# A two-layer hybrid encoder: both layers' Hyena filter networks on two halves of the partitions, and layer 1's decay table made at the end of layer 0

## The chip, the core and the metric

One NeuronCore of one Trainium2 chip runs the whole program. Its engines are TensorE (PE, the matrix products; PEld is its weight load), VectorE (DVE), ScalarE (ACT), GpSimd (POOL) and SyncE (SP, which here only issues DMAs). Each of them works through its own queue in order: an instruction that waits holds up all that stand behind it on the same engine. The metric is device time in microseconds (us) of one execution, lower is better.

## What is computed

The reference runs two layers over two independent requests (s = 0 and 1, 512 tokens of 1024 features each) that share all weights. Cut to what matters here:

```python
def _layer(x, p, ...):
    h = _rmsnorm(x, norm_mix)
    q, k, v, g, hy_in, pool_in = jnp.split(h @ w_in, ...)
    ret = _retention(_rope(q), _rope(k), v, ret_decay_fwd, ret_decay_bwd)   # 4 heads
    ret = _head_layernorm(ret, ret_gn) * jax.nn.silu(g)
    hy_out = _hyena(hy_in, ..., hy_w1, hy_b1, hy_freq, hy_w2, hy_b2, hy_w3, hy_bias)
    pool_out = _pool_mixer(pool_in, pool_w, pool_scale)
    x = x + jnp.concatenate([ret, hy_out, pool_out], axis=-1) @ w_out
    gate, up = jnp.split(_rmsnorm(x, norm_ffn) @ ffn_w_up, 2, axis=-1)
    x = x + (jax.nn.gelu(_dwconv3(gate, ffn_conv)) * up) @ ffn_w_down
    return x + jax.nn.sigmoid(x @ ple_gate_w) * _rmsnorm(p @ ple_w, ple_norm)

def _hyena_filters(L, w1, b1, freq, w2, b2, w3):      # depends on the weights of the layer alone
    h = jnp.sin(fr * (feats @ w1 + b1))               # 512 x 33 @ 33 x 64
    h = jnp.sin(fr * (h @ w2 + b2))                   # 512 x 64 @ 64 x 64
    h = (h @ w3).reshape(L, HY_ORDER, 2, HY_WIDTH) * jnp.exp(-t * deltas)
    k_full = ...; k_full = k_full / jnp.sum(jnp.abs(k_full), axis=0)
    return jnp.fft.rfft(k_full, axis=0)

def _retention(q, k, v, logit_f, logit_b):
    lgf, lgb = log_sigmoid(logit_f), log_sigmoid(logit_b)
    dmask = exp(dist * lgf) below the diagonal, exp(dist * lgb) above     # the decay table
    ...
```

The filters and the decay table of a layer hang on weights alone, so they can be made at any time before the layer uses them.

## The kernel before

Activations lie feature-major, in tiles of 128 features by 512 tokens. A large product splits weights and activations into a high and a low fp16 part and makes three matmuls per 128x128 block (`mm3`, L322 to L324; `pass3`, L327 to L329, for products of activations). Weights come by DMA as `wraw`, and ACT and DVE split them into `wspl` (one instruction on each).

The program is recorded from generators ("threads"): one main thread per request (projections named `q0`..`q3`, `k`, `g`, `hy0`..`hy5`, `pl0`, `pl1`, the output projections `o0`..`o7`, the gated FFN `fg`, `fu`, then a joint FFN `fx`, `fy`, `fz` of both requests, and the per-layer embedding with `pe` and the gate products `s0`..`s7`), one thread per retention head (`sc` scores, `st`/`pt` decayed scores, `ov`, then a head norm with `cs` column sums and `rb` their broadcast), per pooling block (`pu`, `pw`, `pm`, `pq`), per Hyena request, and for each layer one filter thread and one decay thread. `schedule()` steps the thread whose planned time is due; a thread's `ready` is such a planned time, in planned microseconds. What comes out sets the order on PE and on SP. The order on DVE, ACT and POOL is chosen by a list scheduler when the program is built. On the chip all of them are fixed queues.

The two side threads that the change touches:

- `filter_thread(l)`: loads `feats`, the small weights `fw` and `w3`; two products (`fp<-feats,fw` L468 and `fp<-fa,fw` L474, each in 32 bits), each followed by five to seven DVE instructions and a Sin on ACT (`sine`, names `fa`, `sk`); the split `h2`; eight products `fp<-w3s,h` that make `hfb`, `fabs`, `fs`, `fd`, `ftot`; then the sum `fp<-ftot,ones` (L510), its reciprocal `frec` (L512), a block of folds (`fold`, `fold1`, `folds`) and the spectrum products `khat`. Layer 0's thread runs at the start of the program. Layer 1's is spawned when request 0 reaches `pl1` (`EARLY`) in layer 0, and so runs beside the second half of layer 0's mixer.
- `decay_thread(l)`: loads four tables `dpm`, takes `log_sigmoid` of eight numbers (24 DVE instructions on 128x8 and an Exp `yy`), and for eight half tables makes `dect` (two DVE instructions, an Exp on ACT, a store `ddec`). Heads load it back as `dec`.

Sigmoid, Exp, Sin and Gelu need different tables in ACT: a change of function shows as an ACT_TABLE_LOAD.

Of the kernel before, what the change touches and what calls it, by code (L numbers as in the profile page):

```python
# [31 lines left out]
JOINT = 3  # L32
HYW = 256
# [15 lines left out]
EARLY = "pl1"  # L49

# [46 lines left out]
def tile_order():  # L97

    names = ["v00", "v01", "v10", "v11"]
    for h, more in enumerate((["hy0", "hy1", "hy2", "hy3"], ["hy4", "hy5", "pl0"], ["pl1"], [])):  # L100
        names += [f"q{h}", f"k{h}", f"g{h}"] + more
    names += [f"o{m}" for m in range(NB)]
    for j in range(PLAIN):
        names += [f"fg{j}", f"fu{j}"]
    tiles, steps = list(names), list(names)
    pairs = []
# [15 lines left out]
    return tiles + more, steps + more  # L122
# [13 lines left out]


TILES, STEPS = tile_order()
TILE_AT = {n: i for i, n in enumerate(TILES)}
STEP_AT = {n: i for i, n in enumerate(STEPS)}  # L140
NT, NS = len(TILES), len(STEPS)


class Trunk:
# [54 lines left out]
    def plan_weights(self):  # L199
# [3 lines left out]
        for i in range(self.depth * NS):  # L203
            l, name = divmod(i, NS)
            name = STEPS[name]
# [24 lines left out]
    def prep(self, i):  # L230

        while self.wnext < self.need[i]:
            assert self.room()
            self.piece()
        k = i
        while k + 1 < len(self.at):

            frm = min(self.pos) if "." in STEPS[(k + 1) % NS] else i
# [16 lines left out]
    def wtile(self, l, last):  # L255
        self.live.append(l * NS + STEP_AT[last])
        return self.wp.tile([128, 2, 1024], F16, tag="wspl", name="wspl")
# [7 lines left out]
    def raw_names(self, j):  # L265

        return ("fg" + j[1:], "fu" + j[1:]) if j[0] == "f" else ("ea" + j[1:], "eb" + j[1:])
# [40 lines left out]
    def weight(self, l, name, *ss):  # L308
        i = l * NS + STEP_AT[name]
# [122 lines left out]
    def sine(self, a):  # L432

        k = self.g(name="sk")[0:64, :]
# [13 lines left out]
    def filter_thread(self, l, ev):  # L448
        nc, io = self.nc, self.io
        ft = self.g(name="feats")  # L450
        self.load(ft[0:33, :], io["feats"])
        fw = self.g(name="fw")
        self.load(fw[0:64, 0:132], io["fw"][l])
        w3 = []
        for o in range(2):
            w = self.g(name="w3")
            self.load(w[0:64, :], io["w3"][l][:, o * T:(o + 1) * T])
            q = self.g([128, 2, T], F16, name="w3s")
            self.split(q[0:64, 0], q[0:64, 1], w[0:64, :], WS)
# [4 lines left out]
        w1, w2, b1, fr, b2 = fw[0:33, 0:64], fw[0:64, 64:128], fw[0:64, 128:129], fw[0:64, 129:130], fw[0:64, 130:131]  # L464
# [7 lines left out]
        a2 = self.g(name="fa2")  # L472
        p = self.bank(name="fp")
        nc.tensor.matmul(p[0:64, :], w2, a[0:64, :], start=True, stop=True)  # L474
        self.ts(a2[0:64, :], p[0:64, :], b2, fr, ALU.add, ALU.mult)
        self.sine(a2[0:64, :])
        a = None
        h2 = self.g([128, 2, T], F16, name="h2")
        self.split(h2[0:64, 0], h2[0:64, 1], a2[0:64, :])
        yield 0.9, LAT["sin"][l > 0]  # L480
# [380 lines left out]
    def main_thread(self, s):  # L861
# [12 lines left out]
        for l in range(self.depth):  # L874
            vec = self.vec[l]
            h = []
            yield from self.h_steps(s, x, acc, vec[:, V_NMIX:V_NMIX + NB], h)
            x = None
            if s == 0 and l > 0:
                yield [self.ffn[l - 1].over]  # L880
            hw = self.hcw[l]
            mix = [None] * NB
            done = []
            hy, hev = [], [Event() for _ in range(6)]
            v = []
            for name in TILES[:TILE_AT["o0"]]:
                if name[0] == "v":
                    if name[2] == "0":
                        v.append([])
                        ps = self.values_early(l, h, s) if name == "v00" else [None, None]  # L890
                        for tp in range(2):
                            self.values(l, int(name[1]), h, s, tp, v[-1], ps.pop(0))
                            if ps or name != "v00":
                                yield (10.4 if name == "v00" else 5.2), 0.0
                    continue
                if name == "q0" and s == 0 and l > 0:
                    self.load_rope()
                if name == EARLY and s == 0 and l + 1 < self.depth:
                    self.spawn(self.filter_thread(l + 1, self.khat_ev[l + 1]))
                p = self._proj(l, name, h, s)  # L900
                if name[:2] == "hy":
                    if name == "hy0" and s == 0:
                        self.load_dft(l)
                    j = int(name[2])
                    hy.append(self.conv3(p, hw, j, 6))
                    yield 5.15, 0.0
                    hev[j].set(self.clock + 3.0)
                    if j == 0:
                        done.append(Event())
                        self.spawn(self.hyena_thread(l, hy, hev, mix, done[-1]))  # L910
                elif name[:2] == "pl":
                    b = int(name[2])
                    if b == 0:
                        pw = self.g(name="poolw")
                        self.load(pw[:, 0:256], io["poolw"][l])
                    rc = self.g(name="rc")
                    self.load(rc, io["rcnt"][b])
                    m = self.pooling(p, b, rc)
                    yield 5.15, 0.0
                    done.append(Event())  # L920
                    self.spawn(self.pool_thread(l, b, m, None, pw[:, b * 128:(b + 1) * 128], mix, done[-1]))
                elif name[0] == "q":
                    qk = {"q": self.rotate(p)}
                    yield 5.15, 0.0
                elif name[0] == "k":
                    qk["k"] = self.rotate(p)
                    yield 5.15, 0.0
                else:
                    hd = int(name[1])
                    sg = self.g(name="sg")  # L930
                    self.act(sg, p, ACTF.Sigmoid, scale=1.0 / WS)
                    self.stt(sg, p, 1.0 / WS, sg, ALU.mult, ALU.mult)
                    if hd == 0:
                        yield [self.decay_ev[l]]
                    dec = self.dp.tile([128, 896], F32, tag="dec", name="dec")
                    nc.sync.dma_start(out=dec, in_=self.ddec[l, hd])
                    yield 5.15, 0.0
                    done.append(Event())
                    self.spawn(self.head_thread(l, hd, qk, v, sg, dec, mix, done[-1]))
            h = None  # L940
            if s == 1:
                self.rope = None
            yield done
# [96 lines left out]


# [64 lines left out]
    def ffn_joint(self, l, f):  # L1106

        nc, fcw = self.nc, self.fcw[l]
        b11, b21, b22 = f.h[0][0:4], f.h[0][4:8], f.h[1][4:8]
        t1, t2, t3, t4 = f.sums  # L1110
        f.h = f.sums = None
        right = (b11, t1, b21, t2, b22, t3, t4)
        state = {}
        first = STEP_AT[f"f{PLAIN}.0"]
        end = STEP_AT[f"d{len(PARTS) - 1}_0"]
# [362 lines left out]
```

## Time and profile before

| | |
|---|---|
| time, median of 3 runs | 2456.72 us (2451.26 to 2456.94) |
| the profiled execution's own time | 2451.95 us |
| its span, first to last instruction | 2450.2 us |
| mean granted TensorE clock | 0.990 |
| busy PE / DVE / ACT / POOL | 2379.1 / 1779.5 / 1032.3 / 700.8 us |

PE is busy for 97% of the span, so the time is PE's work plus the few places where PE waits. A wait in a row of the timeline stands in brackets behind the instruction that waited: the idle time before it, and what ended it. PEclk in the table of windows is the granted clock as a share of 2.4 GHz: 0.50 is 1.2 GHz.

### The profile page before, as it was taken

The page shows a single profiled execution, that of the slowest core. Times are in us where ns is not written, and L with a number is a line of the kernel's source. Part 1 is how long each engine was busy: PE and PEld are TensorE (multiplying, and loading weights), DVE is VectorE, ACT ScalarE, POOL GpSimd, SP SyncE. Part 2 cuts the span into 40 slices and gives each one's busy share as a digit, 9 for nine tenths or more (in the row PEclk, how much of TensorE's full clock was granted, in tenths as well). Part 3 has the DMA queues.
Part 4 walks back from the last instruction along what each step waited for, and adds up shares of the span by engine and source line. Part 5 has one row for each costly group of instructions (what it writes and reads, how often), then busy time and mean ns, then how long its engine had stood idle before and what let it go on. Part 6 is the DMA issues. An engine that isn't in the chain of part 4 may idle for free.

```text
span 2450.2 us, 30877 instructions
## 1 busy us (share of the span) xinstructions
PE 2379.1 (97%) x12024; PEld 1169.9 (48%) x12024; DVE 1779.5 (73%) x2526; ACT 1032.3 (42%) x1551; POOL 700.8 (29%) x528
## 2 busy tenths in 40 slices
PE   5999989999999999999999999999999999999997
PEld 4544654444444444444456555544444444444443
DVE  7994886968877868866575686554987786886655
ACT  4543334445534435444433343333553543544441
POOL 1213244124233333320121222510423334332011
PEclk8999999999999999999999999999999999999998
DMA  6122020341121121113232111032012112121301
GB/s 226 65 98 63 24 75 21 115 139 38 45 65 59 46 71 53 62 48 112 78 120 108 50 49 53 28 115 65 27 48 65 58 46 69 54 63 48 112 1 69
DMA packets 64363, 168.60 MB, mean 69 GB/s; under 512 B 7574, under 2 KB 13718, under 8 KB 64216
## 3 DMA queue, kind: packets, MB, share of 16 engines
q1 hardware_dynamic: 58312, 156.40, 19.3%
q10 hardware_dynamic: 5904, 10.23, 1.1%
q8 instruction: 94, 1.54, 0.3%
q14 instruction: 53, 0.43, 0.1%
HBM read 152.18 MB, written 14.42 MB: 68 GB/s over the span
## 4 chain that ended last, share of the span: by engine, by line
PE 74%; DVE 13%; issue 3%; ACT 2%; POOL 2%; DMA 0%; POOLq 0%; DVEq 0%; SPq 0%; ACTq 0%
PE fx L1183 13%; PE ex L1183 7%; PE fy L1183 7%; PE ey L1183 4%; PE fz L1183 3%; PE s L322 2%; PE o L323 2%; PE o L324 2%; PE o L322 2%; PE s L323 2%; PE s L324 2%; PE ez L1183 2%; DVE t L174 2%; DVE wspl L171 2%; DVE conv L171 2%
## 5 line engine op out<-in xcount | busy, mean ns | idle before, releaser
L1183 PEld LDWEIGHTS <-wspl 128*128 128x128 f16 x4704 | 461.1, 98 | 566.2 <-issue 13.7
L174 POOL TENSOR_TENSOR wraw<-wraw 128x512 f32<-128x512 f32 (+1 forms) x240 | 344.4, 1435 | 654.8 <-DVE wspl L171 640.7
L168 ACT ACTIVATE wspl<-wraw 128x1024 f16<-128x1024 f32 (+2 forms) x360 | 327.1, 910 | 370.8 <-POOL wraw L174 71.1
L171 DVE SCALAR_TENSOR_TENSOR wspl<-wraw,wspl 128x1024 f16<-128x1024 f32 (+2 forms) x360 | 395.5, 1100 | 82.6 <-ACT wspl L168 81.3
L1183 PE MATMUL fx<-hs,wspl 128*128 128x512 f16 x1368 | 312.3, 382 | 7.7 <-ACT r L168 7.7
L322 PEld LDWEIGHTS <-wspl 128*128 128x128 f16 x1536 | 152.1, 99 | 181.2 <-issue 6.9
L324 PEld LDWEIGHTS <-wspl 128*128 128x128 f16 x1536 | 150.6, 98 | 183.3 <-issue 3.3
L323 PEld LDWEIGHTS <-wspl 128*128 128x128 f16 x1536 | 150.7, 98 | 177.3 <-issue 3.6
L1183 PE MATMUL ex<-at,wspl 128*128 128x512 f16 x846 | 192.7, 379 | 0.0
L174 POOL TENSOR_TENSOR y<-t,mhalf 128x4 f32<-128x4 f32 x30 | 36.3, 1210 | 402.6 <-DVE t L178 402.5
L168 ACT ACTIVATE at<-conv 128x512 f16<-128x512 f32 x142 | 89.4, 629 | 143.7 <-DVE conv L174 111.8
L174 DVE TENSOR_TENSOR at<-conv,at 128x512 f16<-128x512 f32 x142 | 127.1, 896 | 26.2 <-ACT at L168 24.8
L171 DVE SCALAR_TENSOR_TENSOR conv<-r,scaled,conv 128x511 f32<-128x511 f32 x152 | 129.5, 852 | 2.1 <-ACT conv L168 0.4
L1183 PE MATMUL fx<-h,wspl 128*128 128x512 f16 x456 | 104.6, 379 | 0.0
L1183 PE MATMUL fy<-hs,wspl 128*128 128x512 f16 x456 | 104.6, 379 | 0.0
L1183 PE MATMUL fz<-h,wspl 128*128 128x512 f16 x456 | 104.6, 379 | 0.0
L1183 PE MATMUL fy<-h,wspl 128*128 128x512 f16 x456 | 104.6, 379 | 0.0
L168 ACT ACTIVATE sq<-x 128x512 f32<-128x512 f32 x80 | 49.2, 625 | 123.4 <-DVE x L171 66.3
L1183 PE MATMUL ey<-at,wspl 128*128 128x512 f16 x432 | 101.1, 379 | 0.0
L168 ACT ACTIVATE conv<-conv 128x512 f32<-128x512 f32 x88 | 55.3, 629 | 108.2 <-DVE conv L171 107.1
L174 DVE TENSOR_TENSOR acc<-acc,sq 128x512 f32<-128x512 f32 x84 | 62.6, 747 | 48.5 <-ACT sq L168 47.3
L324 PE MATMUL s<-xs,wspl 128*128 128x512 f16 x256 | 97.0, 379 | 0.0
(246 smaller groups left out, 4662.8 us busy)
## 6 DMA issues: line engine op xcount, KB each, us to landing
wraw<-in_w SPq DMA_DIRECT2D x172, 512.0 KB, 3.8
wraw<-in_w SPq DMA_DIRECT2D x48, 384.0 KB, 3.0
x<-in_x SPq DMA_DIRECT2D x32, 256.0 KB, 4.3
dec<-ddec SPq DMA_DIRECT2D x16, 448.0 KB, 4.6
wraw<-in_w SPq DMA_DIRECT2D x16, 256.0 KB, 2.6
xsp<-x ACTq DMA_DIRECT2D x16, 256.0 KB, 2.0
x<-xsp SPq DMA_DIRECT2D x16, 256.0 KB, 5.0
out_y<-out SPq DMA_DIRECT2D x16, 256.0 KB, 2.8
```

Source lines behind the costliest of these rows:

```text
L168: return self.nc.scalar.activation(out=out, in_=in_, func=func, **k)
L171: return self.nc.vector.scalar_tensor_tensor(out=out, in0=in0, scalar=scalar, in1=in1, op0=op0, op1=op1)
L174: return (eng or self.nc.vector).tensor_tensor(out=out, in0=in0, in1=in1, op=op)
L322: self.nc.tensor.matmul(out, wv[:, 0, kb, :], x[:, 0], start=first, stop=False)
L323: self.nc.tensor.matmul(out, wv[:, 0, kb, :], x[:, 1], start=False, stop=False)
L324: self.nc.tensor.matmul(out, wv[:, 1, kb, :], x[:, 0], start=False, stop=last)
L1183: mm = lambda a, b, start=False, stop=False: self.nc.tensor.matmul(out, a, b, start=start, stop=stop, skip_group_check=not first)
```

## The change

Layer 0's filter thread now makes the inner layers of both layers: layer 0 stands on partitions 0 to 63 and layer 1 on 64 to 127 (`fw` holds the two `w1` side by side and the two `w2` as a block diagonal), so the two products and the sines have 128 rows and as many columns as before, and `h2` stays in SBUF until layer 1's thread uses its lower half. Layer 1's filter thread is still spawned at `EARLY`, but begins with the `w3` products. Layer 1's decay thread gets the planned time 25 + 1125 in place of 25 + 400. A main thread that reaches its first head gate no longer gives way to others when the decay table is already there. The bodies of the projections' steps move into a function `take`. The diff also adds a way of running pairs of projections jointly (`TWINS`, `mix_joint`, `rights`); `TWINNED` is empty, so that code is never entered.

```diff
+TWINNED = ()
 EARLY = "pl1"
+LATER = 1125.0
...
     def sine(self, a):
-        k = self.g(name="sk")[0:64, :]
+        k = self.g(name="sk")
...
     def filter_thread(self, l, ev):
         nc, io = self.nc, self.io
-        ft = self.g(name="feats")
-        self.load(ft[0:33, :], io["feats"])
-        fw = self.g(name="fw")
-        self.load(fw[0:64, 0:132], io["fw"][l])
+        rows = slice(l * 64, (l + 1) * 64)
+        if l == 0:
+            ft = self.g(name="feats")
+            self.load(ft[0:33, :], io["feats"])
+            fw = self.g(name="fw")
+            self.load(fw[:, 0:259], io["fw"])
...
-            self.split(q[0:64, 0], q[0:64, 1], w[0:64, :], WS)
+            self.split(q[rows, 0], q[rows, 1], w[rows, :], WS)
...
-        a = self.g(name="fa")
-        p = self.bank(name="fp")
-        nc.tensor.matmul(p[0:64, :], w1, ft[0:33, :], start=True, stop=True)
-        self.ts(a[0:64, :], p[0:64, :], b1, fr, ALU.add, ALU.mult)
-        self.sine(a[0:64, :])
-        yield 0.9, LAT["sin"][l > 0]
...
+        if l == 0:
+            w1, w2, b1, fr, b2 = fw[0:33, 0:128], fw[:, 128:256], fw[:, 256:257], fw[:, 257:258], fw[:, 258:259]
+            a = self.g(name="fa")
+            p = self.bank(name="fp")
+            nc.tensor.matmul(p, w1, ft[0:33, :], start=True, stop=True)
+            self.ts(a, p, b1, fr, ALU.add, ALU.mult)
+            self.sine(a)
+            yield 0.9, LAT["sin"][0]
...
+            self.h2 = self.g([128, 2, T], F16, name="h2")
+            self.split(self.h2[:, 0], self.h2[:, 1], a2)
+            yield 0.9, LAT["sin"][0]
+        h2 = self.h2
...
-                self.pass3(p, h2[0:64, 0, jj], h2[0:64, 1, jj], w3[o][0:64, 0], w3[o][0:64, 1], True, True)
+                self.pass3(p, h2[rows, 0, jj], h2[rows, 1, jj], w3[o][rows, 0], w3[o][rows, 1], True, True)
...
-                    if hd == 0:
-                        yield [self.decay_ev[l]]
...
+            if hd == 0 and self.decay_ev[l].time is None:
+                yield [self.decay_ev[l]]
...
-            self.spawn(self.decay_thread(l, self.decay_ev[l])).ready = 25.0 + 400.0 * l
+            self.spawn(self.decay_thread(l, self.decay_ev[l])).ready = 25.0 + LATER * l
...
-    fw = np.zeros((depth, 64, 132), f4)
+    fw = np.zeros((128, 259), f4)
```

Three places show how the queues move. The first is PE, layer 0, where `pl1` of request 0 ends; before, what stands behind its last matmul is the first of the two small filter products, and then the scores of the next head:

```order
L324 MATMUL pl_3193<-h,wspl 128x512
L468 MATMUL fp<-feats,fw 64x512
L327 LDWEIGHTS qk
L327 MATMUL sc<-qk 128x512
L328 LDWEIGHTS qk
```

And now (L339 to L341 are the three passes of `pass3`):

```order
L336 MATMUL pl_3193<-h,wspl 128x512
L339 LDWEIGHTS h_530
L339 MATMUL fp<-w3s,h_530 128x512
L340 LDWEIGHTS h_530
L340 MATMUL fp<-w3s,h_530 128x512
L341 LDWEIGHTS h_530
L341 MATMUL fp<-w3s,h_530 128x512
L339 LDWEIGHTS qk
L339 MATMUL sc<-qk 128x512
```

The first `w3` product stands where the feature product stood, and it reads `w3s`, which ACT and DVE make. The second place is DVE in layer 0 right after `pl1` of request 1. Before, two heads' decayed scores stand there between the last filter products' sums:

```order
L174 TENSOR_TENSOR qk<-rt,qk 128x512
L174 TENSOR_TENSOR fs_3674<-hfb 128x256
L174 TENSOR_TENSOR fd_3678<-hfb 128x256
L171 SCALAR_TENSOR_TENSOR st<-sc,dec 128x512
L174 TENSOR_TENSOR ftot<-ftot,fabs 128x256
L171 SCALAR_TENSOR_TENSOR st<-sc,dec 128x512
```

Now the reciprocal (L529, directly behind the two `wspl` that stand there), the first head's four `st` and four `pt`, and these rows stand there, ahead of the second head's `st` and `pt`:

```order
L186 TENSOR_TENSOR qk<-rt,qk 128x512
L540 COPY fold_3919<-fold 128x512
L186 TENSOR_TENSOR fold<-fold,frec 128x512
L543 COPY fold<-fd_3258 1x512
L186 TENSOR_TENSOR fold<-fold,frec 128x512 x2
L541 COPY fold_3919<-fold 1x512
L186 TENSOR_TENSOR fold<-fold,frec 128x512 x4
L542 COPY fold<-fs_3252 1x512
L186 TENSOR_TENSOR fold_3919<-fold_3919,frec 128x512
L183 SCALAR_TENSOR_TENSOR st<-sc,dec 128x512
L183 SCALAR_TENSOR_TENSOR folds<-fold,folds 128x512
L186 TENSOR_TENSOR fold<-fold,frec 128x512
```

Before, the reciprocal and this block stood behind the last heads' scores, beside `o0` to `o2`. The third place is ACT at the end of layer 0, from the gate of product `s6` of request 0 to that of `s2` of request 1. Before:

```order
L168 ACTIVATE sg<-s_10223 128x512
L168 ACTIVATE wspl<-wraw 128x1024
L168 ACTIVATE sq<-x 128x512
L184 DMA xsp<-x 128x512 x2
L168 ACTIVATE sq<-x 128x512
L184 DMA xsp<-x 128x512
L168 ACTIVATE sg<-s_10284 128x512
```

And now, behind the gate of `s6`:

```order
L180 ACT_TABLE_LOAD
L180 ACTIVATE dect<-dect 128x448
L196 DMA ddec<-dect 128x448
L180 ACTIVATE wspl<-wraw 128x1024
L180 ACTIVATE dect<-dect 128x448
L196 DMA ddec<-dect 128x448
L180 ACTIVATE sq<-x 128x512
L196 DMA xsp<-x 128x512 x2
L180 ACTIVATE sq<-x 128x512
L196 DMA xsp<-x 128x512
L180 ACT_TABLE_LOAD
L180 ACTIVATE sg<-s_10233 128x512
```

Exp and Sigmoid now alternate there: the program has 22 ACT_TABLE_LOADs in place of 15, three fewer in the mixer of layer 0 and ten more in this stage.

## Rows read from the trace of the kernel before

**Rows 1.** The page, part 1: busy time, share of the span, instructions.
```profile
PE 2379.1 (97%) x12024; PEld 1169.9 (48%) x12024; DVE 1779.5 (73%) x2526; ACT 1032.3 (42%) x1551; POOL 700.8 (29%) x528
```

**Rows 2.** Timeline of PE, its waits: start us, us, instruction, [idle before, releaser].
```profile
44.87 1.87 PE L753 MATMUL cs<-ones,acc 128*128 128x1 f32 x8 [6.57 <-DVE acc L174]
...
333.42 0.38 PE L324 MATMUL pl<-h,wspl 128*128 128x512 f16 x1
333.63 0.38 PE L322 MATMUL pl<-h,wspl 128*128 128x512 f16 x1
...
334.37 1.07 PE L468 MATMUL fp<-feats,fw 33*64 33x512 f32 x2
...
359.26 1.05 PE L753 MATMUL cs<-ones,sq 128*128 128x1 f32 x8 [2.48 <-ACT sq L168]
...
398.08 0.39 PE L327 MATMUL fp<-w3s,h 64*128 64x512 f16 x1
...
422.36 1.05 PE L753 MATMUL cs<-ones,sq 128*128 128x1 f32 x8 [2.75 <-ACT sq L168]
...
466.25 0.56 PE L763 MATMUL rb<-identr,rr 128*128 128x128 f16 x7 [1.33 <-DVE rr L171]
...
1246.30 0.95 PE L753 MATMUL cs<-ones,acc 128*128 128x1 f32 x8
...
1279.41 1.02 PE L753 MATMUL cs<-ones,acc 128*128 128x1 f32 x8 [0.50 <-DVE acc L174]
```

**Rows 3.** Windows: us, then busy time of each engine, PEclk, DMA share, GB/s.
```profile
37.60:51.30 13.70, 7.13 (x35) 5.23 (x34) 12.95 (x25) 4.07 (x7) 2.04 (x1) 0.50 0.55 200
...
423.30:426.70 3.40, 3.40 (x10) 1.17 (x11) 3.16 (x10) 1.81 (x3) 2.13 (x2) 0.50 0.66 217
...
500.00:600.00 100.00, 100.00 (x485) 46.87 (x484) 75.86 (x102) 43.80 (x72) 35.84 (x26) 1.00 0.26 86
```

**Rows 4.** Timeline, behind `pl1` of request 0: the split of `w3`.
```profile
334.97 1.14 ACT L168 ACTIVATE w3s<-w 64x512 f16<-64x512 f32 x2
...
335.62 1.14 DVE L171 SCALAR_TENSOR_TENSOR w3s<-w,w3s 64x512 f16<-64x512 f32 x1 [2.23 <-ACT w3s L168]
```

**Rows 5.** Timeline of DVE, from `pl1` of request 1 to the folds.
```profile
399.76 1.25 DVE L171 SCALAR_TENSOR_TENSOR wspl<-wraw,wspl 128x1024 f16<-128x1024 f32 x1 [1.28 <-ACT wspl L168]
...
406.15 1.77 DVE L174 TENSOR_TENSOR pt<-st,pt 128x512 f16<-128x512 f32 x1
...
415.46 0.69 DVE L174 TENSOR_TENSOR qk<-rt,qk 128x512 f16<-128x512 f32 x1 [2.06 <-ACT qk L168]
...
448.73 3.35 DVE L512 RECIPROCAL frec<-fp 128x512 f32<-128x512 f32 x1
...
460.68 0.41 DVE L526 COPY fold<-fd 1x512 f32<-1x512 f32 x1
...
462.56 1.88 DVE L174 TENSOR_TENSOR fold<-fold,frec 128x512 f32<-128x512 f32 x3
```

**Rows 6.** Timeline of POOL, the pooling block of request 1 and a fold.
```profile
400.00 4.53 POOL L174 TENSOR_TENSOR pw<-pw 128x525 f32<-128x525 f32 x3
...
439.90 1.27 POOL L174 TENSOR_TENSOR fold<-fs,fs 128x512 f32<-128x512 f32 x1
```

**Rows 7.** Timeline of ACT, the square that the third `cs` waits for.
```profile
421.73 0.58 ACT L168 ACTIVATE sq<-ov 128x512 f32<-128x512 f32 x1
```

**Rows 8.** End of layer 0: timeline of ACT and DVE, then the tile `dect` (count, duration ns min/median/max).
```profile
1241.32 0.60 ACT L168 ACTIVATE sg<-s 128x512 f32<-128x512 f32 x1 [0.88 <-PE s L324]
...
1244.80 1.29 DVE L174 TENSOR_TENSOR acc<-acc,sq 128x512 f32<-128x512 f32 x2 [0.70 <-ACT sq L168]
...
L171 DVE SCALAR_TENSOR_TENSOR dect<-dpm,lg,dect x16: 669/676/1690, 83.6 to 515.7; 128x448 f32<-128x448 f32 x16
```

**Rows 9.** Timeline of ACT, a table load and the Sigmoid behind it.
```profile
388.90 1.28 ACT L168 ACT_TABLE_LOAD   x1
390.19 0.60 ACT L168 ACTIVATE sg<-g 128x512 f32<-128x512 f32 x1
```

More of the change, by code (lines that the diff above doesn't have):

```diff
@@ L105, in tile_order @@
     tiles, steps = list(names), list(names)
+    if twinned:
+        both = [n for t in TWINS for n in t]
+        mixing = [n for n in mixing if n not in both]
+        steps = [n for n in steps if n not in both]
+        steps[4:4] = lace([f"m{i}" for i in range(len(TWINS))])
     pairs = []
@@ L121, in tile_order @@
     more = ["p0", "p1"] + [f"s{m}" for m in range(NB)]
-    return tiles + more, steps + more
+    return tiles + more, steps + more, mixing
 def step_time(name):
@@ L895, in main_thread @@
                     continue
+                if l in TWINNED and not M.done.owner and s == 1:
+                    M.done.owner = self
+                    yield [self.decay_ev[l]]
+                    yield from self.mix_joint(l, M)
+                    M.done.set(self.clock)
+                    yield 0.0, 0.0
+                elif l in TWINNED and M.done.time is None:
+                    yield [M.done]
+                if name == EARLY and s == 0 and l + 1 < self.depth:
+                    self.spawn(self.filter_thread(l + 1, self.khat_ev[l + 1]))
@@ L940, in main_thread @@
-            h = None
+                box = [self._proj(l, name, h, s)]
+                yield from self.take(l, s, name, box, M, 5.15)
+            h = M.h[s] = None
             if s == 1:
                 self.rope = None
+            mix, done = M.mix[s], M.ends[s]
             yield done
@@ new lines, in mix_joint @@
+    def mix_joint(self, l, M):
+        right = self.rights(M)
+        state = {}
+        self.load_rope()
+        for _, name in STEPS[STEP_AT[l, "m0.0"]:STEP_AT[l, f"m{len(TWINS) - 1}.6"] + 1]:
+            key, q = name.split(".")
+            q = int(q)
+            w = self.weight(l, name, 0, 1)
+            st = state.setdefault(key, {})
+            if q in (0, 1, 2):
+                st["XYZ"[q]] = self.bank(name="m" + "xyz"[q])
+            p = st["XYZXYXX"[q]]
+            self.product(p, w, right[q], q < 3)
+            i, s, box = 0, 0, []
+            if q in (0, 1, 3):
+                r = st[("r1", "r5", None, "r2")[q]] = self.g(name="r")
+                self.act(r, p)
+                r = None
+            elif q == 6:
+                i, box = 1, [p]
+                del state[key]
+            else:
+                n = {2: "r1", 4: "r2", 5: "r5"}[q]
+                self.tt(st[n], p, st[n], ALU.add)
+                i, s, box = int(q == 5), int(q > 2), [st.pop(n)]
+                if q < 5:
+                    del st["Z" if q == 2 else "Y"]
+            st = p = None
+            if box:
+                yield from self.take(l, s, TWINS[int(key[1:])][i], box, M, 2.58)
+            else:
+                yield 2.58, 0.0
@@ L1108, in ffn_joint @@
         nc, fcw = self.nc, self.fcw[l]
[L1109 to L1112, printed above, removed]
+        right = self.rights(f)
+        f.h = None
         state = {}
-        first = STEP_AT[f"f{PLAIN}.0"]
-        end = STEP_AT[f"d{len(PARTS) - 1}_0"]
-        for name in STEPS[first:end]:
+        first = STEP_AT[l, f"f{PLAIN}.0"]
+        end = STEP_AT[l, f"d{len(PARTS) - 1}_0"]
+        for _, name in STEPS[first:end]:
             j, q = name.split(".")
@@ L1122, in ffn_joint @@
                 st["XYZ"[q]] = self.bank(name=name[0] + "xyz"[q])
-            last = name == STEPS[end - 1]
+            last = name == STEPS[end - 1][1]
             if last:
@@ L1133, in ffn_joint @@
                 self.stt(x, p, 1.0 / (WS * FFS), x)
[L1134 removed]
+                if q == 5 and STEPS[end - 1][1] == f"{j}.6":
                     x = f.x[0][2 * i + 1]
@@ L1243, in run @@
         self.ffn = [Ffn() for _ in range(self.depth)]
+        self.mix = [Mix() for _ in range(self.depth)]
         a = self.spawn(self.main_thread(0))
```

162 lines of the change are left out of this document (88 added, 74 removed).

## The prediction

> **What bounds the kernel now.** The page comes first: PE is busy for 97% of the span [rows 1], so the time changes only where PE's own work changes or where PE waits. The list of PE's waits comes next, and in the timeline each of them with its place and releaser [rows 2]. The reader is to see there which of them lie near the moved work: 2.48 us at 359.26 and 2.75 us at 422.36, both of a `cs` that waits for ACT's square of `ov`, 1.33 us at 466.25 of an `rb` that waits for DVE, and 0.50 us at 1279.41. At 1246.30 a `cs` starts with no wait, and its `acc` was done at 1246.09 (two instructions from 1244.80 in 1.29 us [rows 8]), so there is no slack there either. Last come the windows: from 500 to 600 us PE runs 100.00 of 100.00 us [rows 3], so DVE and ACT work taken out of the output projections relieves nothing beyond the 1.33 us just ahead of them. After a long wait the granted clock falls: from 423.30 to 426.70 it is 0.50, that is 1.2 GHz [rows 3], so a stretch of 3.4 us costs about 1.7 us on top of the 2.75 us wait. The 2.48 us wait has such a stretch behind it too. All sums are made against the profiled execution, 2451.95 us, which is 4.8 us below the median of the three runs; the difference is then set on the median.
>
> **Work that goes away.** Layer 1 no longer makes its two small 32-bit products. The first takes 1.07 us [rows 2] and holds up the next instruction by about 1.0 us; the second is taken as the same: **-2.0 us** of PE. The layer-0 products at the start get twice the rows and as many columns, and the sines on 128 partitions have the same free size; both are taken at their old durations. With layer 1's sines go 15 DVE instructions, two Sins and two changes of table between 334 and 390 us. They stood ahead of the square behind the 2.48 us wait at 359.26. PE now comes there about 1.4 us later (2.4 us of a new wait below, less 1.0), and ACT earlier: I keep 0.3 us of that wait, **-2.2 us** (bounds 0 and -2.5).
>
> **A new wait behind `pl1` of request 0.** PE is free there at 334.37 [rows 2]. Before, the feature product stood there and waited for nothing. Now it is a product with `w3s`, whose split is not moved: ACT's two parts start at 334.97, behind the copy of `pl1`'s result, and DVE's first part runs from 335.62 for 1.14 us [rows 4], so to 336.76. The product waits until then: **+2.4 us** (2.0 to 2.8), and what stands behind it on PE, the scores of the next head, waits too.
>
> **The fold block behind `pl1` of request 1.** This is the largest term. Call P the time at which that `pl1` gives way to the next product on PE (398.08 before [rows 2]). From P, PE has the sum product (about 1.0 us, priced as the other 32-bit products), 12 matmuls of scores, 24 of `q3`, 12 of scores, 12 of `ov` and 24 of `k3`, 84 at 0.215 us (two neighbours start at 333.42 and 333.63 [rows 2]): 18.1 us. PE so reaches the `cs` at P + 19.1. That `cs` needs the square of `ov`, which stands on ACT behind the second head's four `pt` and one `folds`, and the last `pt` needs the second head's last `st` on DVE. Before, those `st` had only filter sums between them. Now DVE must first do this: the two `wspl`, of which the second waits for an ACT part that stands behind the copy of `pl1` (before it began 399.76 and took 1.25 us [rows 5], done at P + 2.9); the reciprocal, 3.35 us [rows 5], to P + 6.2; eight `st`/`pt`, one `rt`, four folds, one `qk`, four COPYs, nine multiplies by `frec`, a `folds` and six `st`/`pt`, that is 30 instructions of 0.62 us (three in 1.88 us) and four of about 0.4 us [rows 5]: 20.2 us. With no wait at all the last `st` ends at P + 26.4, and `pt`, `folds` and the square on ACT, about 0.58 us each [rows 7], bring the `cs` to P + 28.1. That is a wait of 9.0 us. Waits come on top: `qk` waits for ACT and POOL, as at 415.46 with 2.06 us [rows 5]; four folds on POOL at 1.27 us [rows 6] stand behind the rotation, and multiplies wait for them; while POOL pools, 4.53 us and more [rows 6], a `pt` took 1.77 us [rows 5] in place of 0.62. Some of the waits fall together; I add 1.0 us. So 10.0 us (8.5 to 12) in place of 2.75 us: **+7.2 us** (5.7 to 9.3). All that stands behind the `cs` on PE (`ov`, `g3`, the head norms) is late by as much; the output projections then find their inputs ready, so the 1.33 us at 466.25 go: **-1.3 us**.
>
> **The clock.** The slow stretch behind 359.26 goes, and the 2.4 us wait at 334 may bring another in its place. The one behind the second `cs` stays and may grow: around the 6.57 us wait at 44.87 [rows 2] the clock is 0.50 from 37.60 to 51.30 [rows 3], 6.4 us beyond the end of the wait, which is 3.2 us lost where the 2.75 us wait lost 1.7. I take half of that difference, **+0.8 us** (-1.7 to +3).
>
> **The decay table at the end of layer 0.** It adds 24 tiny and 16 larger DVE instructions, nine Exps, eight stores on ACT's queue and ten table loads beside the gate products. DVE and ACT have room, so only the two `cs` count. Ahead of the one at 1246.30, DVE has two more `dect` instructions of 0.68 us [rows 8] in the chain of `e`, `x`, square and `acc`, and ACT has a table load of 1.28 us [rows 9] ahead of the gate at which the last gate's result waits (1241.32 before [rows 8], about 1243.0 now); followed to the end, `acc` comes 0.9 us later, and no slack was left: +0.9. The one at 1279.41 already waited 0.50 us; its chain goes through `hn` and the `wspl` and slides 2 us, PE 1 us: +0.9. Together **+1.8 us** (0 to 5; 0 if the loads fall into ACT's idle time). The next layer reads its `dec` tiles 100 us later, so the later table itself delays nothing.
>
> **The start.** `fw` grows from 33 to 132 KB in a queue that feeds the first activations, whose wait stands at 44.87. At the 200 GB/s of the window there [rows 3] the 99 KB are 0.5 us, the upper bound; part of the activations stands ahead of it, so **+0.3 us** (0 to 0.5). Everything else is the same set of instructions on PE; `q1` of request 0 in layer 1 changes places with four spectrum groups, where nothing waits.
>
> **Sum.** -2.0 - 2.2 + 2.4 + 7.2 - 1.3 + 0.8 + 1.8 + 0.3 = +7.0 us, so 2459.0 us for the profiled execution and **2463.7 us** on the median.
>
> **Rivals.** *The folds don't gate.* If the second head's last `st` ended by P + 17.5, ten us earlier than worked out, the `cs` would not wait: for that 16 of DVE's 34 instructions would have to stand behind it, and its queue is fixed, which speaks against it. Then -2.0 - 2.2 + 2.4 - 2.75 - 1.3 + 1.8 + 0.3 and two slow stretches less (-3.4) make -7.2 us: 2449.5 us on the median, faster.
>
> *Half of it is hidden.* If the block's waits overlap PE's own (the second head's scores need free PSUM banks, and `ov` needs the first head's `pt`), the `cs` stall might be 5 us; the sum is then +2 us, 2458.7 us on the median. Against it: what delays PE ahead of the `cs` is no gain in the total.
>
> *The tables gate the end of layer 0.* If a change of table cost twice its load on the path, 2.56 us, and two of them lay in the chain to each `cs`, the stage would lose 1.8 + 4 x 1.28 = 6.9 us: 2468.8 us. Against it stands the row: the load at 388.90 takes 1.28 us and the Sigmoid behind it starts at 390.19, 0.01 us after its end [rows 9]. The Trainium skill has the same rule with its own price (ScalarE: Activation LUTs, What ACT_TABLE_LOAD costs): a load of about 1.28 us and a drain of about 1.38 us with it, some 2.66 us for every switch to another set. The load agrees with this trace and the drain is not to be seen in it.
>
> **How the numbers follow.** The forecast's mechanism, with a sum between +4 and +11 us, has a chance of 0.50; the folds that don't gate 0.12, half of it hidden 0.18, the tables 0.20. The range goes from 2452 us (half hidden, less half the 5.7 us over which the three runs spread, and part of the way to the first rival) to 2474 us (the tables, with the folds at their upper bound). About 0.3%, 7.4 us, is what a measurement can tell from no change. Slower by more: the tables and 0.45 of the forecast, 0.43. Faster by more: most of the first rival, 0.11. Within: 0.46.
>
> **What the changed profile would show.** Right: a `fp<-w3s` near 335 with a wait of about 2.4 us released by DVE `w3s`; the `cs` at about 359 with next to none; the `cs` behind `k3` of request 1 with some 10 us, released by ACT's square, at 1.2 GHz afterwards; no wait at the `rb` near 466; about 1 us more at each of the two `cs` near 1246 and 1279. It is wrong if that `cs` waits less than 5 us, or if a wait stands anywhere in 500 to 1200 us that was not there, or if the clock stays down for much longer than 6 us.

## The result and the profile after

The changed kernel takes 2468.35 us (median of 6 runs, 2466.87 to 2470.04) against 2454.16 us of the kernel before (6 runs, 2450.15 to 2457.15): 14.2 us more, a ratio of 1.0058 with a 95% interval of 1.0047 to 1.0068. The forecast was +7.0 us, 2463.7 us, in a range of 2452 to 2474 us; the chance given to "slower by more than 0.3%" was 0.43. The profiled execution has a span of 2467.3 us against 2450.2 us, and a granted clock of 0.985 against 0.990.

PE's waits in the changed kernel, from the timeline of PE; these rows answer to [rows 2]:

```profile
337.48 0.37 PE L339 MATMUL fp<-w3s,h 64*128 64x512 f16 x1 [1.33 <-ACT w3s L180]
338.52 0.37 PE L340 MATMUL fp<-w3s,h 64*128 64x512 f16 x1 [0.67 <-DVE w3s L183]
...
363.68 0.95 PE L770 MATMUL cs<-ones,sq 128*128 128x1 f32 x8
...
436.96 1.87 PE L770 MATMUL cs<-ones,sq 128*128 128x1 f32 x8 [15.64 <-ACT sq L180]
...
1257.95 1.87 PE L770 MATMUL cs<-ones,acc 128*128 128x1 f32 x8 [2.82 <-DVE acc L186]
...
1295.41 1.02 PE L770 MATMUL cs<-ones,acc 128*128 128x1 f32 x8 [1.46 <-DVE acc L186]
```

Every place named ahead shows what was named: a wait at the first `w3` product (1.33 + 0.67 us), none at the `cs` that waited 2.48 us before, a long one at the `cs` behind `k3` of request 1, released by ACT's square, and larger ones at the two `cs` at the end of layer 0. The `rb` near 466 has no wait left. The sizes differ, most of all the third, and 1.33 us of the wait at the first `w3` product were for ACT's part of the split, where DVE's alone was named. The windows of PE's clock, with the columns of [rows 3]:

```profile
425.00:437.00 12.00, 0.04 (x1) 0.04 (x1) 11.90 (x22) 4.24 (x8) 0.00 (x0) 0.50 0.11 29
437.00:442.10 5.10, 5.10 (x17) 2.89 (x18) 3.35 (x6) 1.61 (x3) 3.37 (x3) 0.50 0.51 188
1257.90:1264.70 6.80, 6.75 (x20) 3.50 (x21) 6.44 (x12) 5.01 (x7) 3.41 (x2) 0.50 0.36 99
```

The clock is at 1.2 GHz from 425 us on, in the middle of the long wait, while PE does nothing and loses nothing by it; after the wait it stays there for 5.1 us, some 2.5 us lost. Behind the wait at 1257.95 it stays for 6.8 us, 3.4 us lost. Before, the clock is 1.00 from 1246.30 to 1253.10, and no slow stretch stands at the end of layer 0.

Why the third wait is 15.6 us and not 10 is in the timeline of DVE, from the second `wspl` to the first multiply, and the second head's last `st`:

```profile
403.94 1.24 DVE L183 SCALAR_TENSOR_TENSOR wspl<-wraw,wspl 128x1024 f16<-128x1024 f32 x1 [3.89 <-ACT wspl L180]
405.11 3.35 DVE L529 RECIPROCAL frec<-fp 128x512 f32<-128x512 f32 x1
408.38 1.22 DVE L183 SCALAR_TENSOR_TENSOR st<-sc,dec 128x512 f32<-128x512 f32 x2
...
415.28 2.92 DVE L186 TENSOR_TENSOR fold<-fs,fs 128x512 f32<-128x512 f32 x2
418.13 3.42 DVE L186 TENSOR_TENSOR fold<-fd,fd 128x512 f32<-128x512 f32 x2
421.48 1.75 DVE L186 TENSOR_TENSOR qk<-rt,qk 128x512 f16<-128x512 f32 x1
423.15 1.48 DVE L540 COPY fold<-fold 128x512 f32<-128x512 f32 x1
424.55 0.68 DVE L186 TENSOR_TENSOR fold<-fold,frec 128x512 f32<-128x512 f32 x1
...
434.57 0.67 DVE L183 SCALAR_TENSOR_TENSOR st<-sc,dec 128x512 f32<-128x512 f32 x1
```

and of POOL beside it:

```profile
416.06 1.60 POOL L186 TENSOR_TENSOR rt<-rt,sw 128x512 f32<-128x512 f32 x1
417.62 3.39 POOL L186 TENSOR_TENSOR fold<-fs,fs 128x512 f32<-128x512 f32 x2
420.97 3.38 POOL L186 TENSOR_TENSOR fold<-fd,fd 128x512 f32<-128x512 f32 x2
```

Up to the reciprocal all is as worked out: P is 402.2, the reciprocal starts at P + 2.9. Then two of DVE's folds run beside POOL's rotation (`sw` and `rt`), and two more, `qk` and a COPY beside POOL's folds: while POOL is in a `fold` of 1.7 us (1.27 us in [rows 6]), an instruction of DVE takes up to 1.75 us where the sum had 0.62. The multiplies behind POOL's last fold are back at 0.6 us. From the first `st` at 408.38 to the end of the last at 435.24 it is 26.9 us where the sum had 20.2. These 6.7 us are what the wait has more than the 9.0 us that the sum gave without any waits. The page "GPSIMD Engine Reference" of the Trainium skill (1. Specifications) says that GpSimd's interfaces to SBUF are shared with VectorE, with contention for DVE instructions in a 2-port perf mode or with two SBUF inputs. The folds and `qk`, with two inputs, agree. The COPY at 423.15, with one input, is slowed as well (1.48 us for 0.41); whether it runs in such a mode no run here shows.

### The profile page after: what moved, and what is told of

Its sections match the earlier page's. It is cut to its first block, busy times and chain, and to the rows that moved or that the text cites. A ratio compares the mean times of both kernels' runs of the same rounds, so it can differ in the third digit from the quotient of the medians.

```text
span 2467.3 us, 30843 instructions
## 1 busy us (share of the span) xinstructions
PE 2381.9 (97%) x12020; PEld 1173.4 (48%) x12020; DVE 1777.9 (72%) x2511; ACT 1040.3 (42%) x1555; POOL 713.3 (29%) x528
## 4 chain that ended last, share of the span: by engine, by line
PE 70%; DVE 10%; issue 2%; ACT 2%; POOL 0%; POOLq 0%; DVEq 0%; ACTq 0%
PE fx L1255 14%; PE ex L1255 7%; PE fy L1255 7%; PE ey L1255 4%; PE fz L1255 4%; PE o L334 2%; PE o L335 2%; PE o L336 2%; PE ez L1255 2%; PE s L334 2%; PE s L335 2%; PE s L336 2%; DVE conv L183 1%; PE d L334 1%; PE d L335 1%
## 5 line engine op out<-in xcount | busy, mean ns | idle before, releaser
L186 POOL TENSOR_TENSOR wraw<-wraw 128x512 f32<-128x512 f32 (+1 forms) x240 | 353.5, 1473 | 642.6 <-DVE wspl L183 628.5
L183 DVE SCALAR_TENSOR_TENSOR conv<-r,scaled,conv 128x511 f32<-128x511 f32 x152 | 138.7, 913 | 2.1 <-ACT conv L180 0.4
L186 DVE TENSOR_TENSOR at<-conv,at 128x512 f16<-128x512 f32 x142 | 118.5, 836 | 26.8 <-ACT at L180 25.5
L335 PE MATMUL s<-xs,wspl 128*128 128x512 f16 x256 | 98.0, 383 | 0.0
L334 PE MATMUL s<-xs,wspl 128*128 128x512 f16 x256 | 98.0, 383 | 0.0
```

The lines of the kernel that those rows point to most:

```text
L183: return self.nc.vector.scalar_tensor_tensor(out=out, in0=in0, scalar=scalar, in1=in1, op0=op0, op1=op1)
L186: return (eng or self.nc.vector).tensor_tensor(out=out, in0=in0, in1=in1, op=op)
L334: self.nc.tensor.matmul(out, wv[:, 0, kb, :], x[:, 0], start=first, stop=False)
L335: self.nc.tensor.matmul(out, wv[:, 0, kb, :], x[:, 1], start=False, stop=False)
```

## Experiments

All ratios are of means, to the kernel before, run in turn with it on the same chip, with 95% intervals; the times are medians. The kernel before alone spreads over 8.7 us in one series (last section), so a median can stand a few us from where its ratio puts it, and experiments of different series are compared by their ratios. Each edit is to the changed kernel unless it says otherwise.

### Which of the two moves costs what

The decay table back at its old time, all else as changed:

```diff
-LATER = 1125.0
+LATER = 400.0
```

> The changed kernel with layer 1's decay table at its old planned time (25 + 400), the filters as changed. Theory: the move of the decay table costs about 6 us of the 14 (waits of 2.8 and 1.5 us at the two cs at the end of layer 0 in place of 0 and 0.5, and a slow clock stretch of 6.8 us that loses 3.4), so the time falls from 2468.4 to 2461 to 2463 us, the cs of request 0 at the end of layer 0 waits for nothing, the one of request 1 about 0.5 us, and the rb ahead of o3 may wait again for 1 to 1.3 us. Rival, the fold block is all of the loss: the time stays within 2 us of 2468. In both the wait of the cs behind k3 of request 1 stays at 15 to 16 us.

Measured: 2461.99 us, 1.0034 (1.0022 to 1.0046). At the end of layer 0 the first `cs` waits for nothing and the second 0.50 us; the `cs` behind `k3` waits 15.65 us; the `rb` has no wait. By the ratios (1.0058 and 1.0034) the moved table accounts for some 6 of the 14.2 us, give or take 4. Three rows of the profile name it: 2.82 us and 0.96 us of wait and the slow stretch behind 1257.95, 3.4 us lost; the two profiles differ in slow stretches elsewhere too. The rival is out.

The reverse, the kernel before with the decay table alone moved:

```diff
-            self.spawn(self.decay_thread(l, self.decay_ev[l])).ready = 25.0 + 400.0 * l
+            self.spawn(self.decay_thread(l, self.decay_ev[l])).ready = 25.0 + 1125.0 * l
```

> The kernel before with only the decay table of layer 1 moved to 25 + 1125. Theory: it costs what the end of layer 0 showed, waits of about 2.8 and 1.5 us at the two cs and 1.7 to 3.4 us of slow clock, less up to 1.3 us at the rb ahead of o3: 4 to 6 us over before, 2458 to 2461 us. Rival, the table loads hide behind PE and the changed kernel's waits there come from its shifted phase: within 1.5 us of before.

Measured: 2459.0 us, 1.0017 (1.0006 to 1.0029). In median this is the 6 us of the theory, by the ratio some 4 us, but not by its rows. The waits at the end of layer 0 are smaller than in the changed kernel, and no slow stretch stands behind them:

```profile
1252.55 1.05 PE L753 MATMUL cs<-ones,acc 128*128 128x1 f32 x8 [0.90 <-DVE acc L174]
...
1286.04 1.02 PE L753 MATMUL cs<-ones,acc 128*128 128x1 f32 x8 [0.77 <-DVE acc L174]
```

That is +1.2 us. Most of the rest of this execution's difference is clock in places ahead of the moved work; two of them are shown in the last section. So the waits that the moved table brings by itself are 0.9 + 0.3 us, and the 2.82 us of the changed kernel have something more in them. DVE's timeline there shows what, first of the changed kernel, ahead of the `cs`:

```profile
1239.63 1.40 DVE L183 SCALAR_TENSOR_TENSOR e<-e,vec,rb 128x512 f32<-128x512 f32 x2 [1.58 <-PE rb L780]
1240.96 1.25 DVE L183 SCALAR_TENSOR_TENSOR dect<-dpm,lg,dect 128x448 f32<-128x448 f32 x1
1242.13 1.75 DVE L186 TENSOR_TENSOR sg<-sg,e 128x512 f32<-128x512 f32 x1
...
1245.78 0.68 DVE L183 SCALAR_TENSOR_TENSOR dect<-dpm,lg,dect 128x448 f32<-128x448 f32 x1
...
1248.35 1.89 DVE L186 TENSOR_TENSOR x<-x,sg 128x512 f32<-128x512 f32 x3
```

then of the next experiment's kernel, whose waits there are 0.90 and 0.78 us too:

```profile
1232.95 2.06 DVE L183 SCALAR_TENSOR_TENSOR e<-e,vec,rb 128x512 f32<-128x512 f32 x3 [2.23 <-PE rb L780]
...
1238.83 1.89 DVE L186 TENSOR_TENSOR x<-x,sg 128x512 f32<-128x512 f32 x3
...
1244.71 1.27 DVE L183 SCALAR_TENSOR_TENSOR dect<-dpm,lg,dect 128x448 f32<-128x448 f32 x2
1245.90 0.68 DVE L186 TENSOR_TENSOR x<-x,sg 128x512 f32<-128x512 f32 x1
```

The list scheduler put two `dect` between the `e` of the PLE norm in the changed kernel, which delays every `x` and square behind them, and ahead of the last `x` of the chain in the other. From the first `e` to the first `x` 8.7 us pass in the one and 5.9 us in the other. Of these 2.8 us some 1.8 are the two `dect`, and 1.0 is the `sg` at 1242.13, which took 1.75 us while POOL added two `sg` (1240.46, 2.87 us); in the other kernel, where it ran beside POOL's as well, it took 0.68 us.

### The long wait

The sum product, the reciprocal and the folds of layer 1 forty planned us later, where they stood before:

```diff
-    "tot": (7.0, 8.0),
+    "tot": (7.0, 48.0),
```

> The changed kernel with layer 1's sum product, reciprocal and folds 40 planned us later, where they stood before, the decay table as changed. Theory: the 15.6 us wait of the cs behind k3 of request 1 is the fold block ahead of the second head's scores on DVE; with the block later it falls below 2.8 us, and the slow clock behind it to at most 3.4 us. That gives back 13 to 15 us; the rb ahead of o3 may take 1.3 us again: 2454 to 2457 us. Rival, the head's chain is late for another reason (the filter products that now stand earlier, or POOL's pooling): the wait stays above 8 us and the time above 2460 us.

Measured: 2456.23 us, 1.0006 (0.9996 to 1.0017). The long wait is gone, and another has come in the output projections, where the folds now stand ahead of `mixr`:

```profile
422.38 1.05 PE L770 MATMUL cs<-ones,sq 128*128 128x1 f32 x8 [1.65 <-ACT sq L180]
...
473.05 0.50 PE L334 MATMUL o<-mixr,wspl 128*128 128x512 f16 x1 [4.08 <-ACT mixr L180]
```

So the place of the fold block, and not the filter products that now stand earlier, makes the 15.6 us.

POOL's four folds put on DVE, nothing else moved:

```diff
-                self.tt(t, fl(X[k]), fl(X[k + 2]), op, nc.gpsimd if k else None)
+                self.tt(t, fl(X[k]), fl(X[k + 2]), op, nc.gpsimd if k and l == 0 else None)
```

> The changed kernel with the four folds of layer 1 that stood on POOL put on DVE, nothing else moved. Theory, the folds of DVE and POOL slow each other (1.75 us in place of 0.62 on DVE): five DVE instructions at 1.68 us spacing go back to 0.62 and a COPY of 1.48 to 0.4, 6.4 us less, against four more instructions, 2.5 us: the wait of the cs behind k3 falls from 15.6 to about 11.5 us and the time to about 2464 us. Rival, the length of DVE's queue alone sets the wait: it grows by 2.5 us to about 18 us and the time to 2471 us.

Measured: 2468.23 us, 1.0055 (1.0038 to 1.0072), no change in time. But the wait is shorter, with four instructions more in DVE's queue:

```profile
434.94 1.87 PE L770 MATMUL cs<-ones,sq 128*128 128x1 f32 x8 [13.78 <-ACT sq L180]
```

```profile
415.12 2.93 DVE L186 TENSOR_TENSOR fold<-fs,fs 128x512 f32<-128x512 f32 x2
417.98 1.28 DVE L186 TENSOR_TENSOR fold<-fd,fd 128x512 f32<-128x512 f32 x2
419.18 1.28 DVE L186 TENSOR_TENSOR fold<-fs,fs 128x512 f32<-128x512 f32 x2
...
422.19 0.41 DVE L540 COPY fold<-fold 128x512 f32<-128x512 f32 x1
```

The first pair still runs beside POOL's rotation (2.93 us), the others at 0.6 us each, and the COPY at 0.41. That is the contention, shown: the rival, by which the wait grows to 18 us, is out. My 11.5 us was too low because only three of the five slowed instructions, two folds and `qk`, stood beside POOL's folds; the other two folds stood beside its rotation, which stayed. In this profile 1.0 of the 1.9 us went to the second `cs` at the end of layer 0, which waits 2.50 us here for 1.46. The rest is clock: 0.57 and 0.58 in 158 to 162 and 626 to 630 us, where the changed kernel has 1.00, but 1.00 behind the first `cs` at the end of layer 0.

The block left where it is and only paced, so that other work can pass between its parts:

```diff
-            yield 0.0, LAT["pace"][0]
+            yield 0.0, LAT["pace"][0] + 4.0 * l
...
-                yield 0.0, LAT["pace"][1]
+                yield 0.0, LAT["pace"][1] + 4.0 * l
```

> The changed kernel with its sum product, reciprocal and folds where they are, only paced: 4 planned us more behind each fold pair and each multiply of layer 1, so that on DVE seven multiplies, three COPYs and a folds (some 6 us) pass behind the second head's scores. Theory: the wait of the cs behind k3 of request 1 falls by that, from 15.6 to 9 to 10 us, and the time by 6 to 8 us (less slow clock behind it), to 2460 to 2463 us. Rival, the head's chain is set by the first head's part and POOL's pooling: the wait stays above 13 us.

Measured: 2454.53 us, 1.0012 (1.0001 to 1.0023).

```profile
429.20 1.87 PE L770 MATMUL cs<-ones,sq 128*128 128x1 f32 x8 [8.71 <-ACT sq L180]
```

The wait falls by 6.9 us, about the length of what passes behind the second head's `st` (some 6 us were expected): the queue's order is the cause. The time falls by more than was said, some 11 us by the ratios (1.0058 to 1.0012), since the end of layer 0 is scheduled otherwise too: 0.90 and 0.80 us of wait there, and no slow stretch.

### Both moves undone, and better places

Late folds and the old decay table together (`"tot": (7.0, 48.0)`, `LATER = 400.0`); what stays of the change is the shared inner layers:

> The changed kernel with both moves undone: folds of layer 1 40 planned us later and the decay table at 25 + 400; what stays of the change is the shared inner layers (two products, 15 DVE instructions and two Sins less) and the w3 wait. Theory: from the version with the late folds alone (2456.2 us) it gives back the waits of 0.9 and 0.3 us at the end of layer 0 and up to 2 us of slow clock, and may take up to 1.3 us at the rb ahead of o3: 2452 to 2455 us, within 0.1% of before. Rival, the decay table beside o3 to o5 meets the folds on DVE there and the 4.1 us wait of o grows: 2457 us or more.

Measured: 2452.57 us, 0.9993 (0.9985 to 1.0002): no difference from before that can be told. The wait of `o` for `mixr` is 4.73 us here.

Paced folds with the old decay table (`LATER = 400.0`):

> The changed kernel with the paced folds and the decay table at 25 + 400. Theory: from the paced version the end of layer 0 gives back its waits of 0.9 and 0.3 us and up to 2 us of slow clock; the 8.7 us wait of the cs stays: 2450 to 2453 us, 1.0 to 1.000 below before. Rival, the decay table beside o3 to o5 delays the paced folds and their products: new waits there and 2455 us or more.

Measured: 2455.7 us, 1.0000 (0.9991 to 1.0009), where the paced version with the late table had 1.0012. The intervals of the two overlap. The `cs` still waits 8.71 us; the end of layer 0 has only the 0.50 us that it had before. The time stands above the theory's 2450 to 2453 us, but so does the kernel before in this series (2456.66 us), and the rival's new waits are not there.

Paced folds, the old decay table, and the sum product behind the second head's `ov`:

```diff
-    "tot": (7.0, 8.0),
+    "tot": (7.0, 24.0),
```

> As the paced version with the old place of the decay table, and the sum product 16 planned us later, behind the second head's ov, so that the reciprocal and the folds stand behind its scores on DVE. Theory: the cs behind k3 of request 1 waits for less than 3 us and no other wait comes in its place, as the paced folds leave DVE room for mixr: 6 us of wait and 3 us of slow clock less than with the early sum: 2443 to 2448 us, some 0.3% under before. Rival, the wait moves on to o or to the spectrum products, whose table loads come late as with the folds 90 us later: 2452 us or more.

Measured: 2452.92 us, 0.9993 (0.9985 to 1.0002), short of the theory. The `cs` waits for 0.80 us, as said. But 2.55 us come at the next head's scores for `qk`, 1.96 us at `o` for `mixr`, 1.75 us at a `cs` near 539 and 1.87 us at `fg` near 576: in each of the places tried beside the mixer and the output projections, the block's work delays some chain.

The same, with layer 1's filter thread started at `g2`, so that the split of `w3` stands ahead of `pl1`:

```diff
-EARLY = "pl1"
+EARLY = "g2"
...
-        yield 0.0, 0.0
+        yield 0.0, 4.0 * l
```

> As the version with the later, paced folds, with layer 1's filter thread started one projection earlier, at g2 of request 0, and its first product 4 planned us after the start, so that the split of w3 stands ahead of pl1. Theory: the 2.0 us wait at the first w3 product goes or hides in the wait of the cs there (3.3 us): 1 to 3 us less than the version it starts from. Rival, the split on ACT and DVE there delays the cs that stands just ahead by its 1 to 2 us: the same time within 1 us, or more.

Measured: 2450.6 us, 0.9981 (0.9972 to 0.9990), faster than both kernels.

```profile
330.27 1.80 PE L770 MATMUL cs<-ones,sq 128*128 128x1 f32 x8 [4.97 <-ACT sq L180]
...
421.96 1.05 PE L770 MATMUL cs<-ones,sq 128*128 128x1 f32 x8 [0.85 <-ACT sq L180]
...
435.95 0.42 PE L341 MATMUL sc<-qk 128*128 128x512 f16 x1 [2.54 <-DVE qk L186]
```

The `w3` wait is gone; 1.1 us of it shows again at the `cs` just ahead (3.88 us in the version it starts from), as the rival said in part.

And this version with the late decay table (`LATER = 1125.0`):

> The version with the early split and the later, paced folds, with the decay table at 25 + 1125 again. Theory: in this version the moved table costs the two waits at the end of layer 0 alone, 0.9 and 0.3 us more, plus up to 1.7 us of slow clock behind the first, and gains nothing in the output projections: 1 to 3 us over the same version with the table at 25 + 400. Rival one, the cost seen when the table alone was moved (6 us) belongs to the table: 5 us or more. Rival two, room on DVE beside o3 to o5 takes away waits there (2.5 us at sc, 1.8 us at cs): no slower, or faster.

Measured: 2452.21 us, 0.9989 (0.9980 to 0.9998), 0.08% or 2.0 us over the same with the table at its old time, but the intervals of the two overlap. The two `cs` at the end of layer 0 wait 0.90 and 0.78 us for none and 0.50, 1.2 us more, as the theory has it. The waits of the second rival stay (2.55 us at `sc`, 1.88 us at `cs`): the room did not take them away. The times alone do not rule out either rival.

### Two places that failed

The split behind `pl1` made harmless by waiting 8 planned us, and the folds 90 planned us later, beside the last output projections (old decay table):

```diff
-        yield 0.0, 0.0
+        yield 0.0, 8.0 * l
...
-    "tot": (7.0, 8.0),
+    "tot": (7.0, 98.0),
```

> As the version with both moves undone, with layer 1's first w3 product 8 planned us later (behind the split) and the folds 90 planned us later, beside the last output projections. Theory: the two waits that were left go, 2.0 us at the first w3 product and 4.1 us ahead of o with its slow clock stretch of 1.7 us, so 2447 to 2451 us, 2 to 5 us under before. Rival, what PE has there is full and the waits only move on (to fg, fu or fx): 2453 us or more.

Measured: 2481.28 us, 1.0116 (1.0101 to 1.0130), far off.

```profile
600.72 0.61 PE L339 MATMUL fp<-folds,fmat 128*128 128x512 f16 x1 [16.15 <-DMA fmat<-in_fdft]
```

The first product of the folds waits 16 us for its table `fmat`, whose load SP issued only at 598.50 us. The profile puts the 64.0 us for which SP's queue stood still before it down to DVE's `hs`, the split of the FFN's normalised input. `fmat` and the `hn` that `hs` reads share one pool of buffers, so the load probably waited for a buffer, but I did not try it with more of them. Three more waits are longer here than in the version with both moves undone: 3.70 us at the `cs` near 373, 5.17 us at `fg` near 536 and 4.54 us at the `cs` near 549. The first `w3` product waits no more.

The same with the decay table in the joint FFN (`LATER = 700.0`):

> The same with the decay table at 25 + 700, so that its Exps stand in the joint FFN between Gelus and bring their table loads there. Theory: PE waits nowhere in the joint FFN, and ACT has more than half of its time free there, so loads cost nothing where no column sum waits: the same time as with 25 + 400 within 1.5 us. Rival, a change of table costs wherever it stands, since Gelu feeds the FFN products: 5 us or more over it, with waits of fx, ex or the like.

Measured: 2485.67 us, 1.0134 (1.0119 to 1.0150), 4.4 us over the last one.

```profile
840.37 1.86 PE L1255 MATMUL fx<-hs,wspl 128*128 128x512 f16 x4 [3.70 <-ACT r L180]
...
879.42 2.75 PE L1255 MATMUL fx<-hs,wspl 128*128 128x512 f16 x12 [1.89 <-ACT r L180]
```

Between Gelus the Exps and their table loads hold up ACT's copies `r`, and PE waits for a bank: 5.6 us of waits that no row there had before. The theory, that ACT has room, is wrong; the rival's waits are there, at a little less than its 5 us.

## Why the prediction was right, and where its sizes were off

Direction and places were right, and so were the releasers but for ACT's part at the first `w3` product. That the range held the time was in part luck. The forecast's own mechanism was given a sum of +4 to +11 us, and +14.2 us were measured; 2468.35 us is nearly the 2468.8 us of the rival *the tables gate the end of layer 0*, and the range reached up to 2474 us because of it. The parts named for that end make 2471 us (2468.8 and the 2.1 us up to the folds' upper bound). The terms, forecast and measured in the profile (us):

| term | forecast | measured | from |
|---|---|---|---|
| two small products less | -2.0 | -2.0 | they are gone; taken at their duration before |
| `cs` near 359 | -2.2 | -2.5 | no wait at 363.68 |
| first `w3` product | +2.4 | +2.0 | 1.33 + 0.67 |
| `cs` behind `k3` | +7.2 | +12.9 | 15.64 less 2.75 |
| `rb` near 466 | -1.3 | -1.3 | no wait |
| slow clock | +0.8 | about +4 | what the span's +17.1 leaves beside waits and work |
| end of layer 0 | +1.8 | +3.8 | 2.82 + 1.46 less 0.50 |
| start | +0.3 | 0 | the `cs` that started at 44.87 starts at 44.85 |

The term that was most mis-sized is the fold block, 10.0 us with a range of 8.5 to 12, measured 15.6. The queue's order was right, shown by the late folds and by the pacing. The step that failed is "I add 1.0 us" for all waits and for POOL together: the row of a `pt` that took 1.77 us beside POOL [rows 5] was read as an exception, and five DVE instructions of some 1.7 us and a COPY of 1.5 us were the rule as long as POOL rotated and added its folds, some 6 us. The experiment without POOL's folds shows it for those that stood beside them, though it takes back only 1.9 us net; for the two beside the rotation it is read from the rows alone.

The end of layer 0 was sized right as a mechanism (0.90 and 0.77 us where the table alone moves, +0.9 and +0.3 against +0.9 and +0.9 forecast). The prediction had two `dect` of 0.68 us in the chain and followed it to +0.9; in the changed kernel they stand earlier in it, one takes 1.25 us and the `sg` behind it 1.75 us: +2.8. What was said of a drain of ACT's pipeline at each table load, by the page "ScalarE: Activation LUTs" of the Trainium skill (What ACT_TABLE_LOAD costs), finds no support: the waits at the end of layer 0 stay under 1 us where the two `dect` do not stand ahead, as worked out without it. The mechanism of the tables rival is out by the same waits: with the ten loads there, they grow by 1.2 us (6.9 us by the rival), though its time nearly came true.

The clock was read too mildly. A slow stretch followed the 15.6 us wait, as foreseen, with 5.1 us of work in it; one of 6.8 us followed the 2.8 us wait, which was not foreseen. Of the signs of being wrong, two came by their letter: the clock stayed down for 17.1 us (425.0 to 442.1), most of it inside the wait, and one small wait stands between 500 and 1200 us that was not there, 0.68 us at `fg` near 591.

One reading was wrong without harm: of the 15 DVE instructions of the sines only seven stood ahead of the square behind 359.26; the other eight ran from 362.98 on. The wait went all the same.

## What to carry to other kernels

Work that only frees PE of a few matmuls can cost more than it saves by where its followers land: 2 us of products were saved here and 13 us of wait bought, because a block of vector work came to stand ahead of a chain that PE waited for. When a block of work moves on an in-order engine, count what then stands ahead of each chain that ends at PE, at the durations that those instructions have beside what the neighbouring engine does at that time. Pacing such a block, so that other chains pass between its parts, took back some 11 us here (a ratio of 1.0058 to 1.0012) without moving its start, 6.9 us of it in that chain's wait.

## What was not expected of the hardware

VectorE and GpSimd slowed each other when both added 128x512 tiles in SBUF: `qk` took 1.75 us for 0.69 on DVE (2.5 times), a fold 1.7 us for 1.27 on POOL (1.3 times), and even a one-input COPY took 1.48 us for 0.41.

Whether a wait of some 2.75 us is followed by a slow stretch differs between executions of the same instructions. Up to 340 us the kernel before and the one with the decay table alone moved run the same program on PE, and both wait 2.75 us at the same `sp` (294.96 and 293.85). The windows of the kernel before, the first from 1.74 us behind that `sp`:

```profile
296.70:300.10 3.40, 3.40 (x33) 3.04 (x32) 3.31 (x7) 0.62 (x1) 0.96 (x1) 1.00 0.00 0
326.30:333.10 6.80, 6.60 (x27) 3.20 (x28) 5.13 (x13) 1.95 (x5) 1.46 (x1) 0.75 0.64 214
```

and of the other, the first from 1.75 us behind it:

```profile
295.60:299.00 3.40, 3.40 (x18) 2.41 (x17) 2.40 (x6) 0.44 (x1) 0.96 (x1) 0.50 0.00 0
326.30:333.10 6.80, 6.80 (x21) 3.49 (x22) 4.75 (x13) 1.70 (x4) 1.40 (x1) 0.50 0.60 214
```

The first has 1.00 and 0.75 of the clock where the second has 0.50: 18 and 21 matmuls in place of 33 and 27, with the same instructions on PE. Over many executions this spreads a kernel's time: of 27 executions of the kernel before in one series, 12 had a granted clock of 0.990 or 0.991 and took 2451.2 to 2454.0 us, 15 had 0.986 to 0.988 and took 2456.6 to 2459.9 us. A difference of a few us between two kernels can so be a matter of which waits the clock happened to answer, and waits in the trace tell more of a cause than the time does. Whether the moved decay table makes slow stretches elsewhere more frequent, which its 4 to 6 us alone would allow, stays open; in the fastest version it costs 1.2 us of wait, and some 2 us that are not clear of the spread.
